# A hybrid residual block on one core: the issue order as a table in the kernel instead of the scheduler's choice

## The chip, the core and the metric

The kernel runs on one core of a Trainium2 chip. The metric is device time in microseconds (us) of one execution of the whole program. A core has five engines, each with its own queue of instructions that it takes strictly in order: TensorE (PE in the profile, with its weight loads shown apart as PEld), VectorE (DVE), ScalarE (ACT), GpSimd (POOL) and SyncE (SP), which in this kernel issues nearly all loads. Engines wait for one another by semaphores. So the order in which a queue holds its instructions decides what stands behind a wait.

## The reference

One layer on 256 tokens of 1024 channels, in float32. The parts in order, shortened:

```python
h = rmsnorm(x, ffn1_pre_g[l])
x = x + 0.5 * rmsnorm(swiglu(h, ffn1_w_in[l], ffn1_w_down[l]), ffn1_post_g[l])
h = rmsnorm(x, mix_pre_g[l])
q_a, f_a, i_a, g_a, q_b, k_b, v_b, f_b, gates = jnp.split(h @ w_in[l], IN_OFFSETS, axis=-1)
o_a = hgrn2_chunkwise(...)
o_a = rmsnorm(o_a.astype(x.dtype), hg_norm_g[l]) * jax.nn.silu(g_a)
y_a = o_a @ w_branch_a[l]
o_b = fox_attention(...)
y_b = o_b.astype(x.dtype) @ w_branch_b[l]
...
x = x + rmsnorm(y @ w_out[l], mix_post_g[l])
h = rmsnorm(x, mem_pre_g[l])
mem_n = rmsnorm(mem, mem_kv_g[l])
x = x + rmsnorm(mem_cross_attention(h, mem_n, w_mq[l], w_mkv[l], w_mo[l]), mem_post_g[l])
h = rmsnorm(x, ffn2_pre_g[l])
x = x + 0.5 * rmsnorm(swiglu(h, ffn2_w_in[l], ffn2_w_down[l]), ffn2_post_g[l])
```

`swiglu` is a gate and an up projection to 2816 channels, silu(gate) times up, and a down projection. `hgrn2_chunkwise` is a gated linear recurrence of 8 heads in chunks of 64 tokens, `fox_attention` a causal attention of 8 heads with a forget gate. `y` is the sum of both branches, each times a sigmoid gate. The memory attention has 4 heads over 256 memory rows.

## The kernel before, in words

**Numbers.** All products of activations and weights are made in a split form: a tile is divided into a high part in the type fp32r and a low part that is the rest. `load_split` (L144) does it for weights: SyncE loads a raw tile of 128 x 1024 (L151), ScalarE casts it to `hi` (L153), VectorE subtracts to get `lo` (L155). Four raw tiles exist; a raw tile is free for the next load when its `lo` is done. `split` (L172) does the same for data made on the chip (L173, L174). Each product of blocks then takes three matmuls, hi·hi, hi·lo and lo·hi, all issued by the helper `MM` (L99), so that nearly every matmul carries L100 in the profile.

**Stages.** The work goes in this order, with times of the trace: first FFN (0 to 200 us), the mixing projections with the HGRN2 recurrence and the FoX attention (200 to 415), gates, branch projections and `w_out` (to 480), the memory attention with its key, value, query and output projections (to 577), the second FFN (to the end). Both FFNs go over 11 chunks of 256 channels (`ffn`, L427); some pairs of chunks are multiplied by a scheme with fewer products that adds weight blocks first (`act_pair`, L571).

**Between the products.** Data that comes out token by channel must be turned before the next product. This is done on TensorE with an identity: `to_T` (L376, transpose at L385) for the residual stream `xs`, `flush` (L436, transposes at L445) for the activated FFN chunks `at`, which `act_evac` (L448) makes out of a silu on ScalarE (`sg`, L450) and a product on VectorE (`at`, L453 or L455), and `mem_pT` (transposes at L1662) for the softmax weights `pm` of the memory attention (normalised on VectorE at L1652 and L1653). After each sublayer `post` (L401) does the norm and the residual: squares on ScalarE (`ssq`, L293), the root (L316, L317), the product `post` (L416), two small steps (L328, L330), and `xs` in two halves (L421) on VectorE; then `half` (L848) transposes `xs` for the next sublayer.

**The head.** The first eight blocks of weights and of transposed `x` come in tiles `head` (L806, L807) and `raw` (L812). A one-column Silu (L814) loads ScalarE's function table while the first data is under way. For each block ScalarE casts two weight blocks (L828), VectorE makes the high and low part of the data (`hlT`, L370 to L373) and the low parts of the weights (L831), and ScalarE makes a scaled copy `xf` (L832).

**What sets the order.** The kernel is traced once from top to bottom, and the scheduler then chooses, engine by engine, in which order the traced instructions go into the queues. The kernel guides it in three ways: `tc.high_priority()` puts a part first, `tc.issue_after(ins)` keeps a part behind a given instruction, and `after(i)` (L103) does both, with the i-th matmul as the point:

```python
    @contextmanager
    def after(i):

        with tc.high_priority(), tc.issue_after(log[min(i, len(log) - 1)]):
            yield
```

The constants at the top (`L_F1 = 24`, `L_MO = 15`, `M_T = (103, 115)` and the like) are such points, counted in matmuls from the start of a part.

Of the kernel before, what the change touches and what calls it, by code (L numbers as in the profile page):

```python
# [68 lines left out]

_ORDER = [  # L70
# [15 lines left out]
def block_kernel(ctx: ExitStack, tc: tile.TileContext, wts, head_in, gf_in, x_in, mem_in, memT_in, cols, rows, fbias, masks, out):  # L86
    nc = tc.nc
    V, S, G, PE = nc.vector, nc.scalar, nc.gpsimd, nc.tensor

    cp = ctx.enter_context(tc.tile_pool(name="consts", bufs=1))  # L90
# [53 lines left out]
    def load_split(src, n=512, behind=None, parts=None):  # L144

        raw = wp.tile([P, D], F32, tag="raw", name=nm("raw"), bufs=4)
        hi, lo = parts or parts_of()
        r, h, l = raw, hi, lo
        if n < 512:
            r, h, l = (p.rearrange("p (k n) -> p k n", k=2)[:, :, :n] for p in (raw, hi, lo))  # L150
        loads.append(nc.sync.dma_start(r, src).ins)  # L151
        with tc.issue_after(behind[0]) if behind else nullcontext():
            casts.append(S.copy(h, r).ins)  # L153
        with tc.issue_after(behind[1]) if behind else nullcontext():
            los.append(V.tensor_tensor(out=l, in0=r, in1=h.bitcast(F32), op=ALU.subtract).ins)  # L155
        return hi, lo
# [138 lines left out]
    def table(ins):  # L295

        with tc.issue_after(ins):
            S.activation(warm, ones[:, 0:1], AF.Abs_reciprocal_sqrt)
# [128 lines left out]
    def ffn(w_in, w_dn, X, r2, n_tok, i_row, first_half, second_half=None):  # L427
# [8 lines left out]
        def flush(n):  # L436

            if late:
                c = late.pop(0)
                tr = trp()  # L440
                trv = tr.rearrange("p (j t) -> p j t", j=2)
                with after(n):
                    for h in range(2):
                        for j in range(2):
                            PE.transpose(trv[:, j, h * P : (h + 1) * P], ats[c, h][:, j * P : (j + 1) * P], ident)  # L445
                    split(acts[c][:, 0], acts[c][:, 1], trv)
# [87 lines left out]
        def pair_inputs():  # L534
            for k in range(2):
              with tc.issue_after(evs[-1][1]):
                V.tensor_tensor(out=xf[k][:, :, P:], in0=xf[k][:, :, P:], in1=bc(row[:, :P], [P, 4, P], 1), op=ALU.mult)
# [33 lines left out]
        def act_pair(c, between):  # L571
# [55 lines left out]
            with tc.issue_after(last_silu[0]) if c - 2 in pairs else nullcontext():  # L627
                u = splits(sums)
# [14 lines left out]
            with tc.high_priority():  # L643
                t = half_tile("c01")
                V.tensor_tensor(out=t, in0=b4, in1=v, op=ALU.subtract)
                act_evac(t, c, 0)
            product(b1, of("ad"), splits(both), False)
            S.copy(w, b1)
            with tc.high_priority():
                t = half_tile("c11")  # L650
                V.tensor_tensor(out=t, in0=p5, in1=w, op=ALU.subtract)
                act_evac(t, c, 1, r2[0], q)
# [6 lines left out]
            with tc.high_priority():  # L659
                t = half_tile("c00")  # L660
                V.tensor_tensor(out=t, in0=p1, in1=b0, op=ALU.add)
                act_evac(t, c + 1, 0)
# [7 lines left out]
            with tc.high_priority():  # L670
                silu = act_evac(b1, c + 1, 1, r2[0], q)
# [8 lines left out]
        def pair_loads(c):  # L680
            if c in pairs and c not in sums_of_pair:
                with tc.issue_after(loads[-1]):
                    sums_of_pair[c] = sum_load(c, 0, ((0, 0), (0, 1))), sum_load(c, 1, ((0, 1), (1, 1)))
# [17 lines left out]
        if callable(r2):  # L701
# [4 lines left out]
            for c in range(2):  # L706
                acts[c] = m4([P, 2, 2, T], F32R, "act")
                for h in range(2):
                    with tc.issue_after(casts[-1]):
                        silu = act_evac(outs[c][h], c, h)  # L710
# [3 lines left out]
        for c in range(n_tok, NFF):  # L714
# [42 lines left out]
            if c <= 6 <= last:  # L757
                grow = load_row(i_row)
                if first_half:
                    with tc.issue_after(loads[-1]):  # L760
                        nc.sync.dma_start(masks_s, masks)
# [58 lines left out]
    for kb in range(KB):  # L820
# [3 lines left out]
        for c in range(2):  # L824
            hi, lo = (p[:, kb % 2 * 512 : kb % 2 * 512 + 512] for p in cache[_AT["f1_in"] + 4 * c + kb // 2])
            w = heads[kb][:, HX : HX + 512] if c == 0 else raw1[kb // 2][:, kb % 2 * 512 : kb % 2 * 512 + 512]
            with tc.issue_after(lo_last):
                S.copy(hi, w)  # L828
# [5 lines left out]
    def norm_1():  # L834
        with tc.issue_after(loads[X_AT]):
            for h in range(2):
                nc.sync.dma_start(xs[:, h], x_in[:, h])
        with tc.issue_after(loads[-1]):
            nc.sync.dma_start(cols_s, cols)
            nc.sync.dma_start(fb_s, fbias)  # L840
# [42 lines left out]
    with tc.issue_after(iv_last):  # L883
        S.activation(le, le, AF.Exp)
# [220 lines left out]
    def forget(m):  # L1105
        pf = trp()
        with after(m):
            for h in range(2):
                PE.transpose(pf[0:8, h * P : (h + 1) * P], zf[h], ident)
        V.tensor_scalar(out=fz, in0=pf[0:8, :T], scalar1=fb_s, scalar2=None, op0=ALU.add)  # L1110
        V.scalar_tensor_tensor(out=fa, in0=fz, scalar=-1.0, in1=fz, op0=ALU.mult, op1=ALU.max)
        with tc.issue_after(sig_last):
            logs.append(S.activation(fa, fa, AF.Exp, scale=-1.0).ins)
# [37 lines left out]
    with after(r0):  # L1151
        for r in recs:
            r.grow(0)
    for si, ms in enumerate(SETS):
        with after(r0 + R_AT[si]):
            banks = [acc()]
            banks.append(acc() if ms[-1] in (1, 128) else banks[0])
            for j, m in enumerate(ms):
                for r in recs:
                    r.products(m, banks[r.g if m == 128 else j], j == 1)  # L1160
            with tc.issue_after(gf_last[1, 1]) if si == 1 else tc.issue_after(lo_at["k_b", 1]) if ms[-1] == 64 else nullcontext():
                for r in recs:
                    if ms[-1] < 128:
                        r.grow(ms[-1])
            with tc.issue_after(logs[1]) if ms[-1] == 32 else nullcontext():
                for m in ms:
                    for r in recs:
                        r.keep(m, LEVELS.index(m) if m < 64 else None)
        if si == FG:
            with tc.high_priority(), tc.issue_after(recs[1].grown):  # L1170
                forget_sums()
        if si < 2:
            with tc.high_priority(), tc.issue_after(gf_last[R_GROW[si]]):
                for r in recs:
                    r.grow(SETS[si + 1][0])
# [4 lines left out]
    for g in range(2):  # L1180
        kp = [wp.tile([P, D], F32R, tag="extra", name=nm("kp"), bufs=4).rearrange("p (i t) -> p i t", i=4) for _ in range(2)]
        qp = m4([P, 2, 4, P], F32R, n="qp")
        with tc.high_priority():
            for j in range(2):
                i2 = slice(2 * j, 2 * j + 2)
                with tc.issue_after(recs[1].last) if (g, j) == (0, 1) else nullcontext():
                    split(kp[0][:, i2], kp[1][:, i2], kb_[g][:, i2])
            for j in range(2):
                i2 = slice(2 * j, 2 * j + 2)
                split(qp[:, 0, i2], qp[:, 1, i2], qb_[g][:, i2, P:])  # L1190
# [67 lines left out]
    def fox_pT(g, m):  # L1258
        pT0 = m4([P, 4, T], n="pT0")
        pT1 = wp.tile([P, D], F32, tag="extra", name=nm("pT1"), bufs=4)[:, :512].rearrange("p (i s) -> p i s", i=4)  # L1260
        for h, b in ((0, 0), (1, 0), (1, 1)):
            tr = trp()
            with after(m + 5 * b):
                for i in range(4):
                    PE.transpose(tr[:, i * P : (i + 1) * P], ps_[g, h][:, i, b * P : (b + 1) * P], ident)
                trv = tr.rearrange("p (i s) -> p i s", i=4)
                if b == 0:
                    S.copy(pT0[:, :, h * P : (h + 1) * P], trv)
                else:
                    V.tensor_copy(pT1, trv)  # L1270
# [20 lines left out]
    for c in range(2):  # L1291
# [7 lines left out]
        if c == 0:  # L1299
            for h in range(2):  # L1300
                with after(m + F_S):
                    fox_scores(h)
# [4 lines left out]
    def gates(c):  # L1307
# [6 lines left out]
        with tc.issue_after(loads[-1]):  # L1314
            nc.sync.dma_start(brow, rows[4 + c // 2, c % 2 * 512 : c % 2 * 512 + 512].partition_broadcast(P))
# [8 lines left out]
    for h in range(2):  # L1324
        with after(m + L_OA[h]):
            to_T(OA, lambda kb: Gt[h][:, kb * P : (kb + 1) * P], h, G_HG)
# [3 lines left out]
    for g in range(2):  # L1330
        with after(m + F_O[g]):
            fox_out(g)
# [16 lines left out]
    for c in (0, 2, 1, 3):  # L1349
        with tc.issue_after(marks["OB"][0]):  # L1350
            z_last = S.activation(zs[c], zs[c], AF.Sigmoid)
# [4 lines left out]
    def y_T(c, h, m):  # L1356

        tr = trp()
        with after(m):
            for i in range(4):  # L1360
                PE.transpose(tr[:, i * P : (i + 1) * P], zs[c][:, h, i * P : (i + 1) * P], ident)
            hs = slice(h * P, (h + 1) * P)
            split(Y.h[c][:, :, hs], Y.l[c][:, :, hs], tr.rearrange("p (i t) -> p i t", i=4))
# [50 lines left out]
    def branch_pair():  # L1414
# [8 lines left out]
        with tc.issue_after(loads[-1]):  # L1423
            sums, both = pair_load("br_a", 0, 0, "extra"), pair_load("br_a", 0, 1, "extra")
# [17 lines left out]
        with tc.high_priority():  # L1442
            gated(zs[0][:, 0], combined(b4, v))
# [3 lines left out]
        with tc.high_priority():  # L1447
            gated(zs[0][:, 1], combined(p5, w))
# [3 lines left out]
        with tc.high_priority():  # L1452
            gated(zs[1][:, 0], combined(p1, b0, ALU.add))
        yield
        product(b1, of_x(1, 1), splits(sums), False)
        with tc.high_priority():
            gated(zs[1][:, 1], b1)
# [123 lines left out]
    def mem_v():  # L1581
# [10 lines left out]
        with tc.issue_after(loads[-1]):  # L1592
            sums, both = pair_load("mv", 0, 0, "extra"), pair_load("mv", 0, 1, "extra")
# [70 lines left out]
    for h in range(2):  # L1664
        with after(m + M_S[h]):
            mem_scores(h)
# [18 lines left out]
    for h in range(2):  # L1685
        with after(m + M_T[h]):
            mem_pT(h)
    next(values)
    for i in range(2):
        with after(m + M_O[i]):  # L1690
# [122 lines left out]
```

## Time and profile before

| | |
|---|---|
| median of 3 runs | 766.66 us (766.25 to 766.68) |
| the profiled execution | 767.82 us, its span 765.6 us, mean TensorE clock 0.998 |
| weight casts L153 (188) | 190.9 us, 1033 ns each |
| weight low parts L155 (188) | 222.3 us, 1199 ns each |
| moved from HBM | 156.06 MB read, 205 GB/s over the span |
| weight loads `raw` (215 of 512 KB) | 4.6 us from issue to landing |

The busy time of every engine is in the first lines of the page, shown below. A row of the timeline gives the start, the time of the group, the engine, the line, the operation, the tiles written and read, the shape, and how many like instructions in a row it holds. A bracket at its end gives the idle time of that engine just before, and who ended it. Ends of matmuls are modelled: a matmul of 512 columns is recorded as 0.39 us, though the next one starts 0.23 us after it. A row of the chain of waits gives start, duration and the work on the chain.

### The profile page before, as it was taken

To read this page: it belongs to the slowest core of one execution; us is meant where nothing else is said; L and a number is where in the kernel's file an instruction comes from. 1 tells how busy PE (TensorE), PEld (TensorE's weight loads), DVE (VectorE), ACT (ScalarE), POOL (GpSimd) and SP (SyncE) were. 2 spreads that over 40 slices of the span, in tenths; PEclk is the share of its full clock that TensorE was granted. 3 is DMA by queue.
4 is the path that set the end of the run, shared out by engine and by line. 5 is a ranking of instruction groups with operands and counts; after the bars stand their busy time and mean duration, and the time that the engine had idled before them with its cause. 6 is when DMAs were issued, how large, how long until landed. Compare 5 with 4: busy or idle time off the path is not lost.

```text
span 765.6 us, 11756 instructions
## 1 busy us (share of the span) xinstructions
PE 756.7 (99%) x4302; PEld 642.8 (84%) x4302; DVE 664.4 (87%) x982; ACT 521.2 (68%) x841; POOL 33.0 (4%) x56
## 2 busy tenths in 40 slices
PE   9999999999999999999999999999999999999996
PEld 8888888888888998898888888888887888888885
DVE  6799998988678898888689899999979899997973
ACT  8667576688774659667666755875968566675762
POOL 0000000000000100200001000001000100000000
PEclk9999999999999999999999999999999999999999
DMA  9778777674745545835668955586386837868641
GB/s 350 235 259 245 214 239 275 182 252 167 233 158 149 185 137 183 284 128 182 189 220 245 267 183 186 175 286 131 114 291 191 257 108 257 236 222 269 176 131 55
DMA packets 47146, 157.88 MB, mean 206 GB/s; under 512 B 5385, under 2 KB 9105, under 8 KB 47089
## 3 DMA queue, kind: packets, MB, share of 16 engines
q1 hardware_dynamic: 43168, 144.83, 55.5%
q0 software_dynamic: 3488, 11.94, 8.7%
q8 instruction: 33, 0.54, 0.3%
q10 hardware_dynamic: 432, 0.37, 0.2%
q14 instruction: 25, 0.20, 0.1%
HBM read 156.06 MB, written 1.06 MB: 205 GB/s over the span
## 4 chain that ended last, share of the span: by engine, by line
PE 85%; DVE 8%; ACT 2%; DMA 2%; issue 1%; DVEq 0%; ACTq 0%
PE mm L100 45%; PE acc L100 33%; PE tr L100 5%; DVE lo L155 2%; DMA raw<-in_wts_dram 2%; PE tr L445 1%; DVE lo L174 1%; ACT hi L153 1%; PE tr L385 1%; DVE xs L421 1%; DVE sraw L1393 1%; DMA head<-in_head_dram 0%; DVE post L416 0%; DVE sx L174 0%; DVE qm L1578 0%
## 5 line engine op out<-in xcount | busy, mean ns | idle before, releaser
L155 DVE TENSOR_TENSOR lo<-raw,hi 128x1024 fp32r<-128x1024 f32 (+1 forms) x188 | 222.3, 1199 | 29.5 <-ACT hi L153 26.2
L153 ACT CAST hi<-raw 128x1024 fp32r<-128x1024 f32 (+1 forms) x188 | 190.9, 1033 | 50.3 <-DMA raw<-in_wts_dram 29.7
L100 PE MATMUL mm<-hi,hlT 128*128 128x512 f32 (+1 forms) x632 | 191.6, 382 | 0.0
L100 PEld LDWEIGHTS mm<-hi,hlT 128*128 128x128 f32 x632 | 116.7, 188 | 20.2
L100 PE MATMUL mm<-lo,hlT 128*128 128x512 f32 (+1 forms) x316 | 119.1, 381 | 0.0
L100 PE MATMUL acc<-hi,act 128*128 128x512 f32 x352 | 113.6, 390 | 0.0
L173 ACT CAST hi<-sraw 128x1024 fp32r<-128x1024 f32 x80 | 83.3, 1052 | 33.9 <-DVE sraw L596 15.6
L174 DVE TENSOR_TENSOR lo<-sraw,hi 128x1024 fp32r<-128x1024 f32 x80 | 96.1, 1221 | 3.8 <-ACT hi L173 3.4
L100 PE MATMUL mm<-hi,sx 128*128 128x512 f32 x280 | 90.8, 391 | 0.0
L100 PEld LDWEIGHTS acc<-hi,act 128*128 128x128 f32 x352 | 66.2, 188 | 13.4
L100 PE MATMUL acc<-lo,act 128*128 128x512 f32 x176 | 69.5, 395 | 0.0
L100 PEld LDWEIGHTS mm<-lo,hlT 128*128 128x128 f32 x316 | 59.3, 188 | 10.0
L100 PEld LDWEIGHTS mm<-hi,sx 128*128 128x128 f32 x280 | 52.5, 188 | 10.9
L100 PE MATMUL acc<-hlT,hi 128*128 128x512 f32 x240 | 60.7, 394 | 0.0
L100 PE MATMUL mm<-lo,sx 128*128 128x512 f32 x140 | 54.9, 392 | 0.0
L100 PEld LDWEIGHTS acc<-hlT,hi 128*128 128x128 f32 x240 | 43.1, 189 | 7.7 <-DVE hlT L373 0.2
L174 DVE TENSOR_TENSOR lo<-raw,hi 128x1024 fp32r<-128x1024 f32 x32 | 38.6, 1221 | 2.1 <-ACT hi L173 2.0
L173 ACT CAST hi<-raw 128x1024 fp32r<-128x1024 f32 x32 | 33.1, 1053 | 8.5 <-issue 3.1
L100 PEld LDWEIGHTS acc<-lo,act 128*128 128x128 f32 x176 | 33.1, 188 | 6.4
L100 PE MATMUL acc<-lo,hT 128*128 128x512 f32 x96 | 37.8, 393 | 0.0
L100 PE MATMUL acc<-hi,hT 128*128 128x512 f32 x96 | 37.7, 392 | 0.1
L100 PE MATMUL acc<-hi,lT 128*128 128x512 f32 x96 | 37.3, 391 | 0.0
(329 smaller groups left out, 1232.4 us busy)
## 6 DMA issues: line engine op xcount, KB each, us to landing
raw<-in_wts_dram SPq DMA_DIRECT2D x215, 512.0 KB, 4.6
sraw<-in_wts_dram SPq DMA_DIRECT2D x32, 512.0 KB, 6.6
sraw<-in_wts_dram POOLq DMA_DIRECT2D x20, 512.0 KB, 5.9
raw<-in_gf_dram SPq DMA_DIRECT2D x12, 344.0 KB, 3.7
head<-in_head_dram SPq DMA_DIRECT2D x7, 392.0 KB, 6.4
grow<-in_rows_dram SPq DMA_DIRECT2D x4, 512.0 KB, 7.6
xs<-in_x_dram SPq DMA_DIRECT2D x2, 512.0 KB, 7.6
cb<-cd POOLq DMA_DIRECT2D x2, 512.0 KB, 4.9
```

The costliest lines, as they stand in the source:

```text
L100: log.append(PE.matmul(*args, **kw).ins)
L153: casts.append(S.copy(h, r).ins)
L155: los.append(V.tensor_tensor(out=l, in0=r, in1=h.bitcast(F32), op=ALU.subtract).ins)
L173: a = S.copy(hi, src)
L174: b = V.tensor_tensor(out=lo, in0=src, in1=hi.bitcast(F32), op=ALU.subtract)
L385: PE.transpose(blocks[-1][1], src(kb), ident)
L421: summed = V.scalar_tensor_tensor(out=xh, in0=ts[a // 512][:, a % 512 : (b - 1) % 512 + 1], scalar=r, in1=xh, op0=ALU.mult, op1=ALU.add)
L445: PE.transpose(trv[:, j, h * P : (h + 1) * P], ats[c, h][:, j * P : (j + 1) * P], ident)
L1393: V.tensor_tensor(out=x, in0=x, in1=y, op=ALU.add)
```

## The change

A table `ISSUE` is added. For TensorE, VectorE, ScalarE and SyncE it holds the order of all instructions of that engine (3964, 982, 767 and 290; the page counts more on PE and ACT, where some instructions leave two records), written as runs: `114+18` stands for the 18 instructions from number 114 on, counted in the order in which the kernel traces them. The new function `issue`, called at the end of `block_kernel`, ties each instruction to the one ahead of it in the table, by an order that the scheduler must keep and that needs no semaphore. All uses of `after`, `issue_after` and `high_priority` go. GpSimd's 56 instructions are not in the table. No instruction is added, removed or altered.

```diff
+ISSUE = {
+    "PE": (
+        "0+114 154 114+18 155+2 132 157 133+18 158+3 151 161 152+2 162+15 186 177+9 190+3 187+3 193+49 286+2 242+19 288 261+3 289 264+22 290+64 386 354+27 "
...
+    "DVE": (
+        "1+10 0 11+5 17 16 18+2 242 20 26+3 21+3 29+2 24 31+2 34+2 33 25 36 42 37 50 38+2 43 40+2 46+2 44 51 45 67 48+2 52 243 54 53 68 70+2 55 58+2 57 60 72 "
...
+    "Activation": (
+        "0 2+2 6 5 4 8 7 10 9 11 13 12 15 14 18 17 20 22 1 19 26 21 25 23 33 24 34 30 27 29 32 35+2 31 37 16 41 38+2 42 40 52 43+3 28 53 55+2 46+3 57+2 61+2 64 "
...
+    "SP": (
+        "0+9 15 9+2 13 12 11 14 17+2 16 19+3 27 22+4 28 26 29 31+2 30 33+10 45+4 43+2 49+4 55+2 59+2 54 57 61 58 63 62 64+4 53 68+73 142+4 151 141 147+4 152+2 "
...
+    def issue():
+        traced = [i for i in nc.cur_bb.bb.instructions if i.opcode != "TilePoolBoundary"]
+        for name, runs in ISSUE.items():
+            own = [i for i in traced if i.engine == getattr(mybir.EngineType, name)]
+            order = []
+            for run in runs.split():
+                first, _, n = run.partition("+")
+                order += own[int(first) : int(first) + int(n or 1)]
+            assert len(order) == len(own), (name, len(order), len(own))
+            for before, ins in zip(order, order[1:]):
+                tc.add_manual_dep(ins, before.name, mybir.DependencyInfo(mybir.DependencyClass.NoSync, mybir.DependencyReason.DATA))
...
-    @contextmanager
-    def after(i):
-
-        with tc.high_priority(), tc.issue_after(log[min(i, len(log) - 1)]):
-            yield
-
...
-        with tc.issue_after(behind[0]) if behind else nullcontext():
-            casts.append(S.copy(h, r).ins)
-        with tc.issue_after(behind[1]) if behind else nullcontext():
-            los.append(V.tensor_tensor(out=l, in0=r, in1=h.bitcast(F32), op=ALU.subtract).ins)
+        casts.append(S.copy(h, r).ins)
+        los.append(V.tensor_tensor(out=l, in0=r, in1=h.bitcast(F32), op=ALU.subtract).ins)
...
-            with tc.issue_after(lo_last):
-                S.copy(hi, w)
+            S.copy(hi, w)
...
-            with after(m):
-                to_T(X, x_blocks(h), h, g, (i,) if len(ms) == 2 else (0, 1), mm if X is X3 and h else trp)
+            to_T(X, x_blocks(h), h, g, (i,) if len(ms) == 2 else (0, 1), mm if X is X3 and h else trp)
...
     ffn("f2_in", "f2_dn", X4, r4, 2, 3, None, second)
+    issue()
```

More of the change, by code (lines that the diff above doesn't have):

```diff
@@ L441, in flush @@
                 trv = tr.rearrange("p (j t) -> p j t", j=2)
[L442 to L446, printed above, removed]
+                for h in range(2):
+                    for j in range(2):
+                        PE.transpose(trv[:, j, h * P : (h + 1) * P], ats[c, h][:, j * P : (j + 1) * P], ident)
+                split(acts[c][:, 0], acts[c][:, 1], trv)
         def act_evac(ps, c, h, r=None, q=None):
@@ L1182, in block_kernel @@
         qp = m4([P, 2, 4, P], F32R, n="qp")
[L1183 to L1190, printed above, removed]
+        for j in range(2):
+            i2 = slice(2 * j, 2 * j + 2)
+            split(kp[0][:, i2], kp[1][:, i2], kb_[g][:, i2])
+        for j in range(2):
+            i2 = slice(2 * j, 2 * j + 2)
+            split(qp[:, 0, i2], qp[:, 1, i2], qb_[g][:, i2, P:])
         kq.append((kp, qp))
@@ L1262, in fox_pT @@
             tr = trp()
[L1263 to L1270, printed above, removed]
+            for i in range(4):
+                PE.transpose(tr[:, i * P : (i + 1) * P], ps_[g, h][:, i, b * P : (b + 1) * P], ident)
+            trv = tr.rearrange("p (i s) -> p i s", i=4)
+            if b == 0:
+                S.copy(pT0[:, :, h * P : (h + 1) * P], trv)
+            else:
+                V.tensor_copy(pT1, trv)
         pT0s.append(pT0)
@@ L1358, in y_T @@
         tr = trp()
[L1359 to L1363, printed above, removed]
+        for i in range(4):
+            PE.transpose(tr[:, i * P : (i + 1) * P], zs[c][:, h, i * P : (i + 1) * P], ident)
+        hs = slice(h * P, (h + 1) * P)
+        split(Y.h[c][:, :, hs], Y.l[c][:, :, hs], tr.rearrange("p (i t) -> p i t", i=4))
     def pair_block(name, k, n, j):
@@ L1664, in block_kernel @@
     for h in range(2):
[L1665 to L1666 removed]
+        mem_scores(h)
     AO = Pair()
```

147 lines of the change are left out of this document (59 added, 88 removed), and 52 rows, old and new, of the table ISSUE.

## The prediction

> **What bounds the kernel now.** I read the page first, then the chain of waits, then the busy times of single stretches, and last the timeline at each place where TensorE pauses.
>
> ```profile
> span 765.6 us, 11756 instructions
> ## 1 busy us (share of the span) xinstructions
> PE 756.7 (99%) x4302; PEld 642.8 (84%) x4302; DVE 664.4 (87%) x982; ACT 521.2 (68%) x841; POOL 33.0 (4%) x56
> ```
> ```profile
> 415.58 5.44 PE acc L100 x24
> ```
> ```profile
> 460.00:560.00 100.00, 99.68 (x560) 86.36 (x559) 95.74 (x162) 73.72 (x142) 3.47 (x4) 1.00 0.61 185
> 560.00:620.00 60.00, 59.34 (x274) 48.93 (x273) 50.37 (x89) 39.52 (x71) 2.88 (x4) 1.00 0.73 228
> ```
>
> The columns of the last two are the stretch, its length, the busy time of PE, PEld, DVE, ACT and POOL with their instruction counts, the granted TensorE clock (1.00), the DMA share and GB/s. TensorE is busy 99% of the span at full clock: in the chain, 24 matmuls in a row take 5.44 us, 0.227 us each. So an order that adds and removes no instruction can gain only TensorE's pauses, its start, and what follows its last matmul. The busy columns hide part of each pause, since modelled ends overlap the next start. I therefore compare starts: two neighbouring matmuls start 0.227 us apart, and a larger step is a pause. Next to TensorE, VectorE is the scarce engine: 95.7 us of the 100 from 460 on.
>
> **The pauses that the table can take away.** The first stands at the end of the memory attention, where residual `xs` is normalised and transposed.
>
> ```profile
> 572.44 1.05 ACT L153 CAST hi<-raw 128x1024 fp32r<-128x1024 f32 x1 [0.66 <-DMA raw<-in_wts_dram]
> 573.39 0.59 ACT L293 ACTIVATE junk<-acc 128x512 f32<-128x512 f32 x1
> ```
> ```profile
> 573.52 1.23 DVE L155 TENSOR_TENSOR lo<-raw,hi 128x1024 fp32r<-128x1024 f32 x1 [0.49 <-ACT hi L153]
> ...
> 575.70 1.42 DVE L421 SCALAR_TENSOR_TENSOR xs<-post,y,xs 128x512 f32<-128x512 f32 x2
> ```
> ```profile
> 575.55 0.39 PE L100 MATMUL acc<-hi,hT 128*128 128x512 f32 x1
> 576.60 0.63 PE L385 MATMUL tr<-ident,xs 128*128 128x128 f32 x4 [0.66 <-DVE xs L421]
> ```
>
> The transposes start 1.05 us after the last matmul, so 1.05 − 0.227 = 0.82 is lost, waiting for the first of two `xs` (one takes about 0.71). Ahead of it in its queue ScalarE took a weight cast (572.44) before the square of the norm (573.39), and VectorE a weight's lo part (573.52) before the rest of the chain. Reading the table against the traced order, I find the square and its root ahead of that cast, and post, `t`, `y`, `xs` ahead of that lo part, with the transposes three matmuls earlier. Moved up by those steps, the chain ends about 1.2 us earlier, near 575.2, and the transposes' new turn is 575.55 + 0.227 − 3 × 0.227 = 575.1. I count the whole 0.82 as gone, give or take 0.1. Late next is the displaced cast and lo part, which later matmuls read; nothing there is at zero slack by my reading of the producers.
>
> ```profile
> 738.80 0.38 PE L445 MATMUL tr<-ident,at 128*128 128x128 f32 x2
> 739.49 0.44 PE L445 MATMUL tr<-ident,at 128*128 128x128 f32 x2 [0.32 <-DVE at L455]
> ```
> ```profile
> 542.87 0.39 PE L100 MATMUL mm<-lo,sx 128*128 128x512 f32 x1
> 543.50 0.96 PE L1662 MATMUL acc<-ident,pm 128*128 128x128 f32 x7 [0.24 <-DVE sm L1652]
> ```
> ```profile
> 158.64 0.40 PE L100 MATMUL mm<-hi,sx 128*128 128x512 f32 x1
> 159.01 0.44 PE L445 MATMUL tr<-ident,at 128*128 128x128 f32 x2
> ```
>
> At 738.80 two pairs of `at` transposes stand 0.69 apart, of which the pair itself needs 0.22: 0.47 lost. At 542.87 the transposes of the softmax wait for VectorE: 0.63 − 0.227 = 0.40. At 158.64: 0.37 − 0.227 = 0.14. The table puts other matmuls between: the second pair at 739 comes 4 matmuls (0.9 us) later, the softmax's 6 (1.4 us) later, the pair at 159 3 (0.7 us) later. Each move exceeds its wait, and the matmuls that fill the place belong to other tiles and read data that was there. Sum with the first: 0.82 + 0.47 + 0.40 + 0.14 = **1.83 us**.
>
> **The start.**
>
> ```profile
> 1.18 1.28 ACT L814 ACT_TABLE_LOAD   x1 [1.18 <-PEq L1802]
> 2.47 0.20 ACT L814 ACTIVATE warm<-ones 128x1 f32<-128x1 f32 x1
> 4.17 0.51 ACT L832 ACTIVATE xf<-head 128x256 f32<-128x256 f32 x1 [1.50 <-DMA head<-in_head_dram]
> 4.59 0.60 ACT L828 CAST hi<-head 128x512 fp32r<-128x512 f32 x1
> ...
> 6.54 0.62 ACT L828 CAST hi<-head 128x512 fp32r<-128x512 f32 x1 [0.83 <-DMA head<-in_head_dram]
> ```
> ```profile
> 4.56 0.49 DVE L373 SCALAR_TENSOR_TENSOR hlT<-head,hlT 128x256 fp32r<-128x256 f32 x1
> ```
> ```profile
> 5.24 0.50 PE L100 MATMUL acc<-hi,hlT 128*128 128x512 f32 x1 [0.18 <-ACT hi L828]
> ```
>
> The first matmul (5.24) waits for the cast at 4.59, which stood behind `xf`. The table puts the cast first: it could start at 4.17 and end at 4.77. It also needs `hlT`, whose hi part is done when VectorE goes on at 4.56. So TensorE starts 0.4 us earlier. It gains 0.67 if the weight is read before the cast ends fully, and 0.2 if the second block then waits, since its cast is bound by the landing of its data (6.54) and not by order. I take **0.4**. The warm-up Silu moves behind 18 other ScalarE instructions, so its load of 1.28 leaves idle time and enters busy time. TensorE needs 12 × 0.227 = 2.72 us for one block of the head, ScalarE about 2.0 by these rows, so each block leaves 0.7 of cover and two hide the load. Without that cover it costs up to 1.28. The sequence of functions is otherwise unchanged, so no other load is added.
>
> The row shows ACTIVATE at 2.47, right at the end of the load (1.18 + 1.28). The Trainium skill, "ScalarE: Activation LUTs", section "What ACT_TABLE_LOAD costs", gives about 1.28 us for the load and 1.38 more for a drain, 2.66 in all. The trace agrees on the load and shows no drain behind it; by the page the start would lose 2.66 − 1.4 of cover = 1.3 us before its gain of 0.4, and the sum below would be −0.3 instead of −1.6.
>
> **What the spreading costs.** The PE table moves 169 of 3964 instructions, mostly transposes. Before, they stand in 48 unbroken groups, in the table in 105: 54 singles, 27 pairs, the rest longer.
>
> ```profile
> 577.76 0.39 PE L100 MATMUL acc<-lo,hT 128*128 128x512 f32 x1
> 577.99 0.60 PE L385 MATMUL tr<-ident,xs 128*128 128x128 f32 x4
> 578.35 0.48 PE L100 MATMUL acc<-hi,lT 128*128 128x512 f32 x1
> 578.66 0.39 PE L100 MATMUL acc<-hi,hT 128*128 128x512 f32 x1
> ```
> ```profile
> 32.15 0.40 PE L100 MATMUL mm<-lo,hlT 128*128 128x512 f32 x1
> 32.39 0.38 PE L445 MATMUL tr<-ident,at 128*128 128x128 f32 x2
> 32.52 0.48 PE L100 MATMUL mm<-lo,hlT 128*128 128x512 f32 x1
> 32.84 0.38 PE L445 MATMUL tr<-ident,at 128*128 128x128 f32 x2
> ```
>
> From 577.76 to 578.66 lie two matmuls and four transposes: 0.90 − 0.454 = 0.446, or 0.112 each. From 32.15 to 32.84 lie two matmuls and two transposes: 0.69 − 0.454 = 0.236, or 0.118 each. A split of four into two pairs thus costs 2 × 0.236 − 0.446 = 0.026, with the rounding of both rows about as large. A single is not in this trace. The nearest rows bound it: 0.112 if a group has no fixed cost, 0.131 if it grows in a line. So 57 new groups cost 0 to 57 × 0.026 = 1.5 us. I take 0.01 each, **0.6**, since the pair's rows are rounded to 0.01.
>
> **The other queues.** DVE (843 positions changed), ACT (564) and SP (93 of 290) are mostly shifts by a few places; GpSimd's 56 instructions stay with the scheduler. Where a producer comes later its TensorE reader has slack, 17 readers of 3954 having under 0.3 us before. The largest shift is in the memory stage from 460 on, where the weight loads wait:
>
> ```profile
> SPq L151 <- DVE lo L155: 17.3, 6, 10.7
> ```
> ```profile
> 480.52 1.41 DVE L421 SCALAR_TENSOR_TENSOR xs<-post,y,xs 128x512 f32<-128x512 f32 x2
> ```
> ```profile
> 478.99 1.12 PE L100 MATMUL mm<-hlT,lo 128*128 128x256 f32 x8
> ```
>
> SP waited 17.3 us there (460 to 475) for VectorE's lo parts to release the raw buffers. The table takes those lo parts 9 to 11 places earlier, so loads go out some 3 to 4 us earlier (an estimate from about 1.2 us for a lo part, with other work between), and puts the norm of the first half ahead of the memory's splits. I cost this at nothing; its cover is the loads coming early, and the second rival prices the loss of it.
>
> **Sum.** −1.83 − 0.4 + 0.6 = −1.6 us. The profiled run takes 767.82, its span 765.6, so 2.2 lie around it; the span becomes about 764.0 and a profiled run about 766.2. The runs' median of 766.66 is 1.2 below that profiled run; taking the difference off it gives **765.0 us**. Bounds: all of 1.83, 0.67 at the start and free splitting make −2.5; 0.2 less of the pauses, 0.2 at the start and 1.5 for splitting make −0.3.
>
> **The rivals.** (1) *The waits come back elsewhere.* Transposes placed just in time have no slack: at 159 the new turn falls at 159.0 + 0.7 = 159.7, about where I put the end of its `at`. For: 57 more places where TensorE can meet VectorE late, by some 20 ns each (an estimate, a twelfth of the smallest wait above). Against: VectorE's order was rewritten together with TensorE's. 1.1 to 1.5 come back: 766.4.
>
> (2) *The loads don't come earlier.* The X3 transposes move to about 478.99 + 3 × 0.11 = 479.3; if VectorE's queue keeps its times, the first `xs` ends at 480.52 + 0.71 = 481.2 and TensorE waits 2 us: −1.6 + 2.0 gives 767.1, more if a second such wait follows. For: a fixed queue can't step over a lo part whose load is late, and VectorE has only 4.3 us of idle time in 100. Against: the lo parts that free the buffers move up too.
>
> (3) *Singles are dear*, the case that ends slower. If a single's two changes of operand cost what a pair does (0.236 instead of 0.112), 54 singles add 54 × 0.124 = 6.7: −2.2 + 6.7 = +4.5, 771.2. It decides from (2.2 + 1.5)/57 = 0.065 us per new group. For: no single has been seen. Against: going from four to two hardly shows. The Trainium skill, "TensorE: Matmul & The Clock Gate", section "Part 4: PE-mode transpose", gives about 275 ns for one 128 x 128 transpose in a kernel; the trace's starts inside a group are 0.11 apart, so here that can only be a latency; by the page, 54 singles would add 54 × 0.16 = 9 us.
>
> (4) *Singles are cheaper.* 256 columns take about 0.12 us each (478.99, eight in 1.12), so 128 columns alone might take 0.06 and the rest of 0.112 be weight load that a 512-wide neighbour hides: 54 × 0.05 = 2.7 more gain, 761.7. Against: a pair shows nothing of it.
>
> That the change does nothing is excluded: the chain spans each queue's whole list, so the executed order is the table's.
>
> **How the numbers follow.** 0.2% is 1.5 us, about what a measurement of this kernel can tell from no change; the borders are 765.1 and 768.2. Forecast 0.58, of it 0.36 below 765.1, since pauses under 0.14 that I did not count can only add, and 0.22 above. Rival 1 0.12 (same). Rival 2 0.09 (0.05 same, 0.04 slower). Rival 3 0.08 (slower). Rival 4 0.08 (faster). Unseen 0.05: 0.03 faster, 0.02 slower. Faster 0.47, same 0.39, slower 0.14. A range from 763.2 to 767.4 holds the forecast with its bounds, rival 1 and the first half of rival 2, and leaves out rivals 3 and 4.
>
> **What would show it.** Right: no bracket of idle time ahead of the transposes near 543, 576 and 739; the first matmul at 4.6 to 4.9; steps of about 0.34 from the matmul ahead of a single to the one behind; at 576 the square ahead of the cast; raw loads 3 to 4 us earlier near 470. Wrong: new idle brackets on TensorE over 0.3 us, above all near 479 (rival 2); steps of 0.45 around singles (rival 3) or 0.29 (rival 4); the table load ahead of a cast that TensorE waits for.

## The result: slower by 0.7%

With the table the kernel takes 772.77 us (median of 6 runs, 771.12 to 774.88), the kernel before 766.67 in the same series (766.25 to 769.86). The ratio is 1.007, 95% interval 1.0048 to 1.0093. The forecast of 765.0 is wrong, in sign too, and the range up to 767.4 does not hold the time.

The page of the changed kernel (its line numbers are some 70 higher at the helpers: L100 is now L179, L445 is L514, L385 is L455; in experiments with a shorter table they are up to 9 lower again):

```profile
span 770.9 us, 11756 instructions
## 1 busy us (share of the span) xinstructions
PE 759.1 (98%) x4302; PEld 642.0 (83%) x4302; DVE 660.9 (86%) x982; ACT 515.9 (67%) x842; POOL 32.5 (4%) x56
```

The profiled execution takes 772.72 us. TensorE has the same matmuls as before, so the 5.3 us of span lie between their starts. I look for them as in the prediction, by starts of neighbouring matmuls. Two stand out that the kernel before does not have.

**The first, at 48 us**, is a pair of `at` transposes that waits for VectorE (timeline of TensorE, then of VectorE):

```profile
45.05 0.27 PE L514 MATMUL tr<-ident,at 128*128 128x128 f32 x1
47.99 0.33 PE L514 MATMUL tr<-ident,at 128*128 128x128 f32 x1 [2.67 <-DVE at L522]
```
```profile
39.23 0.42 DVE L522 TENSOR_TENSOR at<-mm,sg 128x256 f32<-128x256 f32 x1
46.31 1.29 DVE L605 TENSOR_TENSOR xf<-xf,row 128x512 f32<-128x512 f32 x2 [6.65 <-DMA row<-rd]
47.52 0.42 DVE L522 TENSOR_TENSOR at<-mm,sg 128x256 f32<-128x256 f32 x1
```

TensorE loses 2.94 − 0.11 = 2.83 us. It waits for an `at` of 0.42 us that depends on nothing late. But VectorE stood still for 6.65 us with `xf`·`row` at the head of its queue, and the `at` is behind it. The `row` is the factor of the norm, spread over all partitions: VectorE turns it (`runs`, L430), and GpSimd sends it to memory and back as `row` (L432, L434). GpSimd's timeline, after and before:

```profile
33.25 0.71 POOL L432 DMA_DIRECT2D rd<-runs  x1 [31.67 <-DVE at L522]
39.90 0.59 POOL L434 DMA_DIRECT2D row<-rd  x1 [5.94 <-DMA rd<-runs]
```
```profile
25.45 0.71 POOL L362 DMA_DIRECT2D rd<-runs  x1 [23.87 <-DVE runs L360]
27.45 0.59 POOL L364 DMA_DIRECT2D row<-rd  x1 [1.29 <-DMA rd<-runs]
```

The first transfer goes out 7.8 us later, since the table has mixed six weight lo parts and two `at` into the 20 short steps that lead to `runs`. And GpSimd then waits 5.94 us for it instead of 1.29. In the kernel before it falls into a lull of the loads (a DMA share of 0.37 from 25 to 29 us; 0.71 with the table), which the traces of runs_early and row_ok, with the chain in one piece, show too (0.36). The stretches in which it starts, after and before (the last two columns are DMA share and GB/s):

```profile
33.00:37.00 4.00, 4.00 (x21) 3.33 (x20) 2.66 (x6) 3.24 (x5) 0.71 (x1) 1.00 0.89 298
```
```profile
25.00:29.00 4.00, 4.00 (x20) 3.30 (x19) 4.00 (x5) 2.89 (x6) 1.30 (x2) 1.00 0.37 130
```

The second transfer is no slower: from issue to landing it took 6.8 us before and takes 6.4 now. So the row lands at 46.3 us instead of about 34; 7.8 us of this come from the late issue and 4.65 from the first transfer. In the kernel before it is there well ahead of its first use at 42.42. And the table has the readers one place ahead of the `at`, where the kernel before had them behind it:

```profile
42.09 0.42 DVE L453 TENSOR_TENSOR at<-mm,sg 128x256 f32<-128x256 f32 x1
42.42 1.28 DVE L537 TENSOR_TENSOR xf<-xf,row 128x512 f32<-128x512 f32 x2
```

Behind this pause the granted TensorE clock falls to half (the column ahead of the DMA share):

```profile
44.00:48.00 4.00, 1.32 (x8) 0.80 (x6) 1.69 (x4) 1.23 (x2) 0.00 (x0) 1.00 0.58 237
...
49.50:53.00 3.50, 3.50 (x10) 2.73 (x9) 3.50 (x5) 0.62 (x1) 0.00 (x0) 0.52 0.49 150
53.00:57.00 4.00, 4.00 (x20) 3.24 (x19) 4.00 (x5) 1.42 (x2) 0.89 (x1) 1.00 0.39 135
```

In 3.5 us at 0.52 TensorE does the work of 1.8: another 1.7 us are lost.

**The second, at 464 us**, has the same form, with the memory's row:

```profile
461.98 0.39 PE L179 MATMUL acc<-hi,hT 128*128 128x512 f32 x1
464.04 0.63 PE L1399 MATMUL tr<-ident,zg 128*128 128x128 f32 x4 [1.68 <-DVE zg L1450]
```
```profile
462.21 0.48 DVE L1538 SCALAR_TENSOR_TENSOR memT<-memT,cols_s,row 128x256 f32<-128x256 f32 x1 [3.14 <-DMA row<-rd]
462.62 0.68 DVE L1446 TENSOR_TENSOR zg<-mm,zg 128x512 f32<-128x512 f32 x1
463.22 0.68 DVE L1450 TENSOR_TENSOR zg<-zg,zg 128x512 f32<-128x512 f32 x1
```

It loses 2.06 − 0.23 = 1.83 us. VectorE waits 3.14 us for the row with `memT`·`row` at the head, and the gated sum `zg` (L1450) that the transposes need stands behind it, though its data was there (in both_first, below, it runs without a wait). In the kernel before `memT` waited for its row too, but this `zg` (there L1412) had run ahead of it:

```profile
449.54 0.68 DVE L1412 TENSOR_TENSOR zg<-zg,zg 128x512 f32<-128x512 f32 x1
456.44 0.88 DVE L1505 SCALAR_TENSOR_TENSOR memT<-memT,cols_s,row 128x256 f32<-128x256 f32 x2 [1.62 <-DMA row<-rd]
```

**What the table does bring is there as well.** The four pauses of the prediction are gone, for example at the end of the memory attention and at 743 us (no bracket ahead of the transposes):

```profile
580.87 0.39 PE L179 MATMUL acc<-hi,hT 128*128 128x512 f32 x1
581.10 0.60 PE L455 MATMUL tr<-ident,xs 128*128 128x128 f32 x4
```
```profile
742.50 0.39 PE L179 MATMUL acc<-hi,act 128*128 128x512 f32 x1
742.73 0.60 PE L514 MATMUL tr<-ident,at 128*128 128x128 f32 x4
```

The start is 0.19 us earlier in this trace: the first product starts at 5.05 instead of 5.24, since now the 20 warm-up matmuls are what ends last ahead of it.

```profile
0.79 4.50 PE L179 MATMUL tr<-const-float32-1.0 128*128 128x128 f32 x20 [0.79 <-PEq L1832]
5.05 1.17 PE L179 MATMUL acc<-hi,hlT 128*128 128x512 f32 x4
```

And a single transpose can be timed now:

```profile
41.94 0.39 PE L179 MATMUL acc<-hi,act 128*128 128x512 f32 x1
42.17 0.27 PE L514 MATMUL tr<-ident,at 128*128 128x128 f32 x1
42.19 0.47 PE L179 MATMUL acc<-hi,act 128*128 128x512 f32 x1
42.51 0.39 PE L179 MATMUL acc<-lo,act 128*128 128x512 f32 x1
```

0.57 − 0.454 = 0.116 us, the 0.112 of one in a group of four within the rounding of the rows.

ScalarE's load of a function table did move. The one at 1.19 us now belongs to the first cast (L887), and the warm-up Silu brings its own at 14.38, in the middle of the work. ScalarE has 14 such loads instead of 13, one of 1.28 us more. No pause of TensorE follows it.

```profile
14.38 1.28 ACT L874 ACT_TABLE_LOAD   x1
15.67 0.20 ACT L874 ACTIVATE warm<-ones 128x1 f32<-128x1 f32 x1
```

The sum: +2.83 +1.7 +1.83 for the two new pauses and the half clock, −1.83 for the four that went, −0.19 at the start, and +1.1 for the spreading (measured below): +5.4, of 5.3 found in the span.

### The profile page after: what moved, and what is told of

Its sections match the earlier page's. It is cut to its first block, busy times and chain, and to the rows that moved or that the text cites. A ratio compares the mean times of both kernels' runs of the same rounds, so it can differ in the third digit from the quotient of the medians.

```text
span 770.9 us, 11756 instructions
## 1 busy us (share of the span) xinstructions
PE 759.1 (98%) x4302; PEld 642.0 (83%) x4302; DVE 660.9 (86%) x982; ACT 515.9 (67%) x842; POOL 32.5 (4%) x56
## 4 chain that ended last, share of the span: by engine, by line
PE 92%; DVE 3%; DMA 2%; issue 2%; ACT 1%; POOL 0%; DVEq 0%; ACTq 0%; POOLq 0%
PE mm L179 45%; PE acc L179 38%; PE tr L179 6%; DMA row<-rd 2%; PE tr L514 1%; DMA rd<-runs 1%; PE tr L455 1%; DVE lo L226 1%; ACT hi L225 1%; PE tr L1309 0%; ACT hi L244 0%; DVE lo L245 0%; ACT junk L364 0%; DVE zg L1446 0%; PE acc L1694 0%
## 5 line engine op out<-in xcount | busy, mean ns | idle before, releaser
L179 PE MATMUL mm<-hi,hlT 128*128 128x512 f32 (+1 forms) x632 | 195.6, 387 | 0.0
L179 PEld LDWEIGHTS mm<-hi,hlT 128*128 128x128 f32 x632 | 116.5, 189 | 20.7
L179 PE MATMUL mm<-lo,hlT 128*128 128x512 f32 (+1 forms) x316 | 120.2, 385 | 0.0
L179 PE MATMUL acc<-hi,act 128*128 128x512 f32 x352 | 114.9, 393 | 0.0
L179 PE MATMUL mm<-hi,sx 128*128 128x512 f32 x280 | 90.8, 392 | 0.0
L179 PEld LDWEIGHTS acc<-hi,act 128*128 128x128 f32 x352 | 65.9, 188 | 13.7
L179 PE MATMUL acc<-lo,act 128*128 128x512 f32 x176 | 69.3, 394 | 0.0
L179 PEld LDWEIGHTS mm<-lo,hlT 128*128 128x128 f32 x316 | 59.8, 189 | 10.1
L179 PEld LDWEIGHTS mm<-hi,sx 128*128 128x128 f32 x280 | 52.4, 188 | 10.8
L179 PE MATMUL acc<-hlT,hi 128*128 128x512 f32 x240 | 60.9, 394 | 0.0
L179 PE MATMUL mm<-lo,sx 128*128 128x512 f32 x140 | 54.9, 392 | 0.0
L179 PEld LDWEIGHTS acc<-hlT,hi 128*128 128x128 f32 x240 | 43.0, 189 | 7.7
L179 PEld LDWEIGHTS acc<-lo,act 128*128 128x128 f32 x176 | 33.1, 188 | 7.1
L179 PE MATMUL acc<-hi,hT 128*128 128x512 f32 x96 | 37.8, 394 | 0.1
L179 PE MATMUL acc<-lo,hT 128*128 128x512 f32 x96 | 37.8, 393 | 0.0
L179 PE MATMUL acc<-hi,lT 128*128 128x512 f32 x96 | 37.4, 392 | 0.0
L179 PEld LDWEIGHTS acc<-hlT,lo 128*128 128x128 f32 x240 | 32.8, 190 | 2.4
```

What stands on the lines that cost most here:

```text
L179: log.append(PE.matmul(*args, **kw).ins)
```

## The experiments

All are edits of the tables, shown in part and with the runs of numbers of VectorE's table written out. The numbers are places in its traced order: 58 and 59 are the two `xf`·`row`, 57 is the `at` behind them, 26 to 41 and 46 to 49 are the chain to `runs` (49), 25, 42 to 45, 67, 72, 73, 76 and 77 are lo parts of weights, 587 is the first `memT`·`row`, 575, 576, 581 and 582 are steps of `zg`. On the chips of these runs the kernel before took 767.95 or 767.96 in the median, 1.3 us more than in the series of the result. So each ratio is to the kernel before of its own series, and runs of different series are compared by their ratios.

**The `at` alone goes ahead of the readers.**

```diff
-68 70 71 55 58 59 57 60 72
+68 70 71 55 57 58 59 60 72
```

> One swap in VectorE's table: the product at that the transposes at 48 us wait for goes ahead of the two products xf*row, which wait for the broadcast row until 46.3 us. Theory A (head of the queue): TensorE's pause there (2.84 us) and the half clock behind it (1.58) are owed only to the place of those two readers; both go, and the time falls by 4.4 to about 768.3 us (767.5 to 769.3). Theory B (the late row): VectorE is still blocked until 46.3 and all that stands behind it stays some 7 us late, so the pause returns at one of the next readers within 15 us, and the time stays at 771 to 773.

772.2 us, ratio 1.0058 (1.0045 to 1.0071). Theory A fell. VectorE still stood still, and the pause came back as three (1.2, 0.9 and 1.1 us, the last at 59.8), which wait for two lo parts and an `at` further back in the queue:

```profile
40.85 0.42 DVE L522 TENSOR_TENSOR at<-mm,sg 128x256 f32<-128x256 f32 x1 [0.43 <-ACT sg L519]
46.44 1.29 DVE L605 TENSOR_TENSOR xf<-xf,row 128x512 f32<-128x512 f32 x2 [5.17 <-DMA row<-rd]
```
```profile
49.65 0.50 PE L179 MATMUL mm<-lo,hlT 128*128 128x512 f32 x1 [1.04 <-DVE lo L226]
51.99 0.50 PE L179 MATMUL mm<-lo,hlT 128*128 128x512 f32 x1 [0.68 <-DVE lo L226]
```

In this run no half clock followed.

**The same, and `zg` ahead of `memT`.**

```diff
-594 587 581 575 576 583 582
+594 575 576 581 582 587 583
```

> The swap of at_first, and four instructions of the gated sum zg put ahead of the first memT*row, which waits for its row until 462.2 us. Theory A: the second pause (1.84) goes as well: 772.7 - 4.4 - 1.8 = 766.5 us (765.5 to 767.3). What is left against the kernel before is then -1.85 for its four pauses, -0.2 at the start, +0.2 at 227 us and +0.5 to +1.0 for split transposes: 0.3 to 1.3 below it. Theory B: 771 or more, with pauses moved to later readers.

770.94 us, ratio 1.0041 (1.0028 to 1.0053). The pause at 464 us is gone from the trace, which settles its cause, and 1.3 us from the time; the first remains (1.5, 0.9 and 1.1 us). So theory A holds where the whole of what TensorE needs is moved ahead, and B's account holds for the first place.

**The row earlier, its readers left.**

```diff
-33 25 36 42 37 50 38 39 43 40 41 46 47 44 51 45 67 48 49 52
+33 36 37 38 39 40 41 46 47 48 49 25 42 50 43 44 51 45 67 52
```

> The other half of the same wait: the chain of small VectorE steps that makes the row (to the turn of runs) is put ahead of the six weight lo parts and at products that the table had mixed into it; the readers of the row stay where the table has them. The row's first transfer is then issued at about 26.5 us instead of 33.3. Theory A: the row lands at about 39 if its two transfers stay as slow as now (5.9 and 6.4 us), 35 if they are as quick as before; the readers stand at the head at about 39.7, so no pause: about 768.3 us. Theory C (contention): the transfers wait for the weight loads whenever they are issued; the row lands at 42 or later and part of the pause stays, 769 to 771.

768.4 us, ratio 1.0008 (0.9997 to 1.002). Against the table's 1.007 that is 0.62% or 4.8 us less, near the 4.4 expected. With the chain in one piece the lull is back, and the first transfer is quick (1.68 us of waiting); theory C fell.

```profile
26.57 0.71 POOL L432 DMA_DIRECT2D rd<-runs  x1 [24.99 <-DVE runs L430]
28.96 0.59 POOL L434 DMA_DIRECT2D row<-rd  x1 [1.68 <-DMA rd<-runs]
```

The readers run at 42.33 without a wait and no pause follows there; a new one of 0.56 at 26.9 is owed to lo part 25, which the edit made late, and the one at `zg` (1.8) is still there.

**The old order, with only the readers ahead of the `at`.**

```diff
-55 72 57 58 59 73
+55 72 58 59 57 73
```

> The kernel before's order as a table on all four engines, with only the two xf*row ahead of that at, as the new table has them. Theory A: the reader's place costs only if the row is late; here it lands at 34 us, and they run at about 42: no difference, 766.7 us (766.2 to 767.3). If the place of the reader alone cost the pause, 769 to 771. If a table as such costs or gains something, that shows here too, as a difference over the whole span without a new pause.

767.67 us, ratio 1.0004 (0.9992 to 1.0016): no difference. So a table as such shows no cost, and the readers' place shows none while the row is early.

**Both rows put right.**

```diff
-33 25 36 42 37 50 38 39 43 40 41 46 47 44 51 45 67 48 49 52
+33 25 36 37 38 39 40 41 46 47 48 49 42 50 43 44 51 45 67 52
-594 587 581 575 576 583 582
+594 575 576 581 582 587 583
```

> The new table with both rows put right: the chain to runs_74 in one piece (behind the last lo part of the head, which the first attempt made late by 0.56 us), and the four zg steps ahead of the first memT*row. Theory D (a late row blocks VectorE's queue): against the run of runs_early (768.4) the pauses of 0.56 and 1.78 us go, 766.1 us (765.3 to 767.0), and no pause over 0.3 us is left on TensorE. If the rows are not the whole cause, it stays at 767.5 or above.

766.97 us, ratio 0.9988 (0.998 to 0.9997). TensorE has no pause over 0.3 us left after the start. So the two rows are the whole of the loss; what remains is a gain of 0.1%, less than the 0.2% forecast.

**And the transposes together again.** In TensorE's table each group that stood together before is joined at the place of its last member. The beginning:

```diff
-0+114 154 114+18 155+2 132 157 133+18 158+3 151 161 152+2 162+15 186 177+9 190+3
+0+132 154+2 132 156+2 133+19 158+4 152+2 162+24 190+3
```

> row_ok with TensorE's table changed in one respect: transposes that stood together before and that the table spreads are put together again at the place of the last of them (51 unbroken groups instead of 105). If spreading costs 0.02 us per new group, as the sums of small steps in the traces so far suggest (9.0 against 7.9 us outside the pauses), it is 1.0 us faster than row_ok, 765.1; by my predicted 0.01, 0.6 faster; if spreading keeps VectorE and ScalarE better fed, pauses return and it is 0.5 to 2 slower.

765.86 us (765.4 to 766.65), ratio 0.9972 (0.9962 to 0.9982): 1.1 below the last, and faster than both kernels. All four old pauses stay away. So spreading costs 0.02 us for each of the 54 groups saved, and it bought nothing here. By the traces about half of that is the change of operand: a single between two matmuls of 512 columns takes 0.12 us in the median of row_ok, where one in a group takes 0.109 to 0.112. The rest stands in a few dear places, a single of 0.27 at most, as small waits would.

**The old order, with the end of the chain late.**

```diff
-46 193 47 48 49 42 43 44 45 50 51 52 53 67 54
+46 193 47 42 43 44 45 50 51 52 53 67 48 49 54
```

> The kernel before's order on all engines, with one thing changed: the last two steps of the chain (the reciprocal and the turn to runs) stand behind the six weight lo parts and at products that the new table has ahead of them. The row is issued at about 32.5 us. Theory D: its first transfer meets loads at a DMA share of 0.9 and takes 5 us instead of 1.3, the row lands at about 45, VectorE stands still from 42.4 on, and TensorE pauses 1 to 3 us between 45 and 62: 768 to 770, though the reader stands behind its at as before. If the reader's place or the rest of the new order is needed as well, no difference: 766.3 to 767.5.

768.43 us, ratio 1.0003 (0.9992 to 1.0014): the expected loss did not come. (The edit puts the two steps behind five lo parts and four `at`, not behind six lo parts.) GpSimd waited 3.28 us for the first transfer, the row landed at 44.5, and VectorE stood still for 1.96, which the old order took without a pause of TensorE before 80 us; some of 0.2 to 0.5 stand later, which this run does not tie to the row.

```profile
33.42 0.71 POOL L423 DMA_DIRECT2D rd<-runs  x1 [31.84 <-DVE runs L421]
37.41 0.59 POOL L425 DMA_DIRECT2D row<-rd  x1 [3.28 <-DMA rd<-runs]
```

**The row late, but ready work ahead of its readers.**

```diff
-55 58 59 57 60 72 61 62 73 76 77 78
+55 57 72 73 76 77 58 59 60 61 62 78
```

> The new table; the row is left as late as it is (46.3 us). The at and the next four weight lo parts (lo_122, lo_125, lo_141, lo_143), whose casts end by about 44.2, go ahead of the two xf*row that wait for it. at_first had moved the at alone, and VectorE still stood still for 5.2 us. Theory E (head of the queue): the harm is what stands behind the waiting readers, not the row's lateness as such; VectorE now fills the wait, the pauses of 2.84 us and the half clock go, 768.3 us (767.5 to 769.3). Theory F (the row itself is on the path): the pair's sums sx that are made of xf*row come too late for TensorE however the rest is placed; 770 to 772.

768.8 us, ratio 1.0017 (0.9998 to 1.0037). The row is as late as ever, and the pause is gone:

```profile
44.34 2.35 DVE L245 TENSOR_TENSOR lo<-sraw,hi 128x1024 fp32r<-128x1024 f32 x2
46.88 1.29 DVE L605 TENSOR_TENSOR xf<-xf,row 128x512 f32<-128x512 f32 x2 [0.19 <-DMA row<-rd]
```

This tells theory E from F: the late row harms only through what stands behind its reader. at_first had moved too little.

**The end of the chain earlier by two lo parts.**

```diff
-51 45 67 48 49 52
+51 48 49 45 67 52
```

> The new table with the last two steps of the chain moved ahead of two weight lo parts only, so that runs is made near 30.3 us instead of 32.7. The first transfer still starts in the busy stretch (DMA share 0.9). Theory E, by dose: VectorE's standstill was 0 (runs_early), 2.0 (old_runs_late), 5.2 and 5.4 (at_first, both_first) and 6.7 us (the new table), with 0, 0, 3.2, 3.4 and 2.8 us of pauses (and in the last 1.6 of half clock). At 2.4 us less than 6.7, so about 4.3, TensorE pauses 0.5 to 2 us, the clock stays whole, and the time is 769 to 770.5. If the first transfer still lands at the same time (it waits for the same loads), the pause and the time stay: 772 to 773.

768.2 us, ratio 1.001 (0.9996 to 1.0023). I had expected half the harm at the first place to stay; none did. Issued 1.4 us earlier, the row is read 5.9 us earlier, without a wait:

```profile
31.85 0.71 POOL L432 DMA_DIRECT2D rd<-runs  x1 [30.27 <-DVE runs L430]
35.68 0.59 POOL L434 DMA_DIRECT2D row<-rd  x1 [3.12 <-DMA rd<-runs]
```
```profile
40.45 1.28 DVE L605 TENSOR_TENSOR xf<-xf,row 128x512 f32<-128x512 f32 x2
```

So the waiting for the first transfer is not a matter of the stretch being busy alone: 3.12 us here, 5.94 in the table, both at DMA shares of 0.89 and more, and 1.68 in the lull of runs_early. Which weight loads a transfer meets was not measured.

**The tables of row_ok, old order on TensorE.** The beginning:

```diff
-0+114 154 114+18 155+2 132 157 133+18 158+3 151 161 152+2 162+15 186 177+9 190+3
+0+129 154+2 129 156+2 130+22 158+4 152+2 162+22 186+4 184+2 190+94
```

> row_ok on VectorE, ScalarE and SyncE with TensorE in the kernel before's order (48 groups of transposes). Against row_ok_joined (765.9), which differs by where whole groups of transposes stand: if moving them away from their producers is what ended the four pauses, pauses at 159, 543, 576 and 739 us return, 1.0 to 1.8 us: 767 to 767.7. If VectorE's and ScalarE's new order ended them, it is level with row_ok_joined, 765.4 to 766.4.

775.98 us, ratio 1.0105 (1.0089 to 1.0122): neither expectation. Not four pauses but some fourteen over 0.2 us stand in it, the largest 2.4:

```profile
88.21 0.44 PE L510 MATMUL tr<-ident,at 128*128 128x128 f32 x2 [2.21 <-DVE at L520]
```

The new order of VectorE makes `at`, and some other tiles, later than the old order of TensorE asks for them: the tables belong together, and the moves of whole groups of transposes are needed, their spreading is not.

## Why the prediction was wrong

- **The four pauses, 1.83 us: right.** All of them are gone, in the table and in row_ok_joined. In old_xf_first, which has the old order, the one at 576 was missing too in its profiled run, so its 0.82 is not lost in each execution.
- **The start: right in sign, one bound left out.** 0.4 forecast, 0.19 measured in the table. I took the cast for the only bound and did not look at the warm-up matmuls, which hold TensorE until 5.05. In the profiled runs with the same head the first product starts at 4.66 to 5.05, 0.2 to 0.6 earlier than before, and the warm-up takes 4.08 to 4.61. "No other load is added" was wrong: one is, and the warm-up's moves into busy time as expected. The cover that I counted on hid it.
- **The spreading: mis-sized, within its bounds.** 0.6 forecast (0 to 1.5), 1.1 measured. The 0.01 for each group was about right; what it left out is small waits, the mechanism of rival 1, of which some 0.5 came and not 1.1 to 1.5. Rival 3 (dear singles) gave 771.2, near the result, but by a mechanism that the trace denies: a single costs 0.116, not 0.236. Rival 4 (cheaper singles) falls by the same row.
- **Rival 2 (late loads stop VectorE at 479 us): wrong place.** The X3 transposes have no bracket. The loads near 470 do come earlier, 1.2 to 3.2 us in row_ok (3 to 4 forecast); in the table, where TensorE is late there by its first pause, it does not show. Its mechanism, a fixed queue that can't step over an instruction whose data is late, is the one that decided, at 46 and 462 us and for a row instead of a weight.
- **The step that failed** is "Where a producer comes later its TensorE reader has slack" under the other queues. I held each later producer against the TensorE instruction that reads its result at last, and the row's sums had slack there. I did not list what stands behind the row's reader in VectorE's own queue: the `at` that TensorE wanted at 45 us, and the lo parts and the `at` that it wanted at 49, 51 and 59 us in at_first. Nor did I ask what the row's first transfer costs in a stretch with the DMA share at 0.89; the trace of before shows it only in a lull at 0.37. The cost of this step was put at nothing; it was 6.4 us by the trace, 2.83 + 1.7 + 1.83, and 6.3 by the ratios of the table and row_ok.
- **The net without this step** would have been −1.83 − 0.19 + 1.1 = −0.9, a ratio of 0.9988; row_ok measures 0.9988 (the 1.1 is itself taken from row_ok, against row_ok_joined). So even then the change would have been too small to tell by the 0.2% of the prediction, and my 765.0 too low by 0.7.

## What to carry to other kernels

When an order is fixed by hand, check each instruction that reads something from a DMA for what stands behind it in the same queue, not only for who reads its result: ready work belongs ahead of it. Keep a chain of short steps that ends in a transfer in one piece; the big steps that fill its gaps delay the transfer, and with the chain in one piece its transfer met fewer loads. Move a group of transposes as a whole.

## What the runs showed of the hardware

A pause of TensorE can cost more than its length, but not always. The traces record the granted clock. In all twelve the stretches at full clock last a whole number of times 3.413 us (in the table 13 times, then 210 times), and a half clock between two of them lasts 3.413 us. So within a run the clock changes on a fixed grid of 3.413 us, wherever a pause begins. Here are the two windows of the grid around the 2.83 us at 48 us in the table, around the 2.37 in row_ok_old_pe, and around the 2.86 at `zg` in runs_mid (the number behind the comma is TensorE's busy time, the third from the end its clock):

```profile
46.02:49.44 3.42, 1.45 (x8) 1.23 (x9) 3.13 (x5) 0.62 (x1) 0.00 (x0) 1.00 0.09 35
49.44:52.85 3.41, 3.41 (x10) 2.64 (x9) 3.41 (x5) 0.62 (x1) 0.00 (x0) 0.50 0.48 151
```
```profile
85.15:88.57 3.42, 1.21 (x8) 0.83 (x7) 3.42 (x5) 3.29 (x5) 0.00 (x0) 1.00 0.91 353
88.57:91.98 3.41, 3.41 (x10) 2.63 (x9) 3.39 (x5) 2.10 (x3) 0.00 (x0) 0.50 0.54 185
```
```profile
457.46:460.87 3.41, 1.51 (x7) 0.93 (x5) 1.03 (x3) 0.00 (x0) 0.00 (x0) 1.00 0.93 366
460.87:464.29 3.42, 2.62 (x14) 2.25 (x15) 3.42 (x8) 1.50 (x3) 0.00 (x0) 1.00 0.09 35
```

The pause of 2.86 is the longest, and behind it the clock stays whole. By busy time, each drop in the twelve traces follows a window with 1.45 us or less, and no window with 1.51 or more is followed by one. But this rests on modelled ends: by starts, the idle time in the first window is 1.97 us in the table and 2.06 in runs_mid, the other way round. So what decides about a drop is not settled here.

The Trainium skill, "TensorE: Matmul & The Clock Gate", section "Part 1: The HAM clock gate (the "warmup" mystery)", states that the clock is set by free-running windows of 3413 ns, and that an idle window halves it until a busy one has passed. The traces agree on the 3.413 us, on the half and on its length, but the windows ahead of the two drops were not idle throughout: TensorE was busy for 1.45 and 1.21 us of them. Its section "Why this matters for your kernels" advises to avoid idle gaps over about 3 us; here gaps of 2.8 and 2.4 us were enough, and one of 2.9 did nothing.

The pause at `zg` differs from one profiled run to the next: 1.8, 1.9, 1.1 and 2.9 us in the table, at_first, readers_late and runs_mid, at the same order around it. Runs with it spread more, 766.64 to 773.49 in readers_late against 766.35 to 767.57 in row_ok, which has no such pause. The two slowest of readers_late also show the lowest granted clock of its ten runs (0.995 and 0.996, the others 0.998 or 0.999), as a half clock behind the pause would. That the landing of a small transfer among large loads is what varies is argued from this, not shown.
